# Both directions' state increments made in one block, the second one in a PSUM bank of the transposes

## The chip, the cores and the metric

One Trainium2 chip, one NeuronCore. The metric is the device time of one execution in microseconds. A core has TensorE (PE; its weight loads are PEld), VectorE (DVE), ScalarE (ACT), GpSimd (POOL) and SyncE (SP, whose queue issues the transfers). PSUM has eight banks, in which TensorE leaves its products.

## The reference

One layer of an encoder over 1024 and 512 tokens of width 1024. After an RMS norm one projection gives the columns of three mixers, whose outputs are joined and projected by w_out. The change lies in the third, a gated linear recurrence with four heads, run forwards and backwards and summed:

```python
def step(state, inp):
    qt, kt, vt, bt = inp                      # a chunk of tokens
    o = (einsum('bhts,bhsv->bhtv', scores, vt)
         + einsum('bhtk,bhkv->bhtv', qt * exp(bt), state))
    state = (exp(b_last)[..., None] * state
             + einsum('bhsk,bhsv->bhkv', kt * exp(b_last - bt), vt))
    return state, o
```

`o_f` runs over the tokens in order, `o_b` over the flipped ones; o = rmsnorm(o_f + o_b), times a gate.

## The kernel before, in words

**Tiling.** The 1536 tokens are three groups of 512. Groups 0 and 1 are one sequence, group 2 is another. In each of the four heads a group is a *unit*, made in the order 2, 0, 1 (`UNITS`). A unit has four chunks of 128 tokens (`NCH`). Projections (`project`, `project_tokens`; tiles pf, pq, pg, pi) are chains of matmuls of a high and a low part.

**Steps.** The code walks through the projections, and after every three matmuls of 512 columns (or six of 256) calls `step()`. It advances a clock by one and resumes those generators that are due. A generator's `yield n` means: resume n steps later. So the small work of the recurrence is put between projection matmuls, in an order fixed when the kernel is built.

**Who keeps that order.** A tile framework adds the semaphores and orders each engine's instructions by its own estimate of when they are ready. In the part with the four heads VectorE alone is held to the order of the code (`manual_schedule`). That part ends with the last gate projection of head 3, after which the output projection (tiles po, yh, yl, yx) begins.

**A unit's generators.** `scores` makes the product of queries and keys inside a chunk by levels m = 1, 2, 4, ... 64. Each level has matmuls (L819, L880; tiles sd, sc), a mask copy (L866 into L, L884 into A), updates of Q, K and T on VectorE (L794, L811), and copies kc, q on ScalarE (L800, L830). It yields 3 steps, then 5 four times, then 1. The next unit's `scores` begins one step after.

`states` first transposes the keys of both directions (tile tk, PSUM tag tp, two banks; copied to kt by ScalarE, L913), yields 4, then makes the increments: per chunk a matmul of keys and values, into a PSUM tile U. `advance` (L925, L928) chains them into the states S on VectorE, the factors coming from `tot` (L905). U's tag is uo, which has one bank. The forward increments are consumed first; `yield 3`; then the backward ones. If the unit isn't the last of its sequence, its last forward increment and its backward ones are copied aside (`keep`, `ub`) by ScalarE; if it is the last, the backward chain runs over all units of the sequence. In both cases the tiles are read by VectorE or ScalarE.

`output` starts 6 steps after the second increments: the product o (L986, the same bank uo), four squares on ScalarE (L991), an inverse root on GpSimd (tile sto, L118 and L119), and the normalised `on` on VectorE (L993). Eight steps later, if the gate G is there, it transposes `on` into a tile `to` (L999, tag tp) and VectorE multiplies by G into yc (L1001), which is stored.

In unit 2 of each head the states and output lie beside the scores of unit 0; in unit 1 no scores run.

**At the end of head 3** the tiles that held the group's activations are reused: the two halves of w_out are loaded into them as each gate projection is done with them (`load_w_out`), then the rows yx of the output projection (L1050).

**The other lines in the rows.** L776 is the gate G. L124 on GpSimd makes the low part wl of a weight, L791 the sum ks of the keys.

Of the kernel before, what the change touches and what calls it, by code (L numbers as in the profile page):

```python
# [15 lines left out]
AF = mybir.ActivationFunctionType  # L16
# [8 lines left out]
NCH = GRP // P  # L25
# [29 lines left out]
def trunk_kernel(ctx, tc, x_prompt, x_sample, norm_g, w_in, conv_w, conv_b, conv_ln_g, conv_ln_b,  # L55
# [3 lines left out]
    act = nc.scalar.activation  # L59
# [21 lines left out]
    def tp_t(name):  # L81
        return ps_tp.tile([P, GRP], F32, tag="tp", name=name)
# [7 lines left out]
    def uo_t(name):  # L90
        return ps_uo.tile([P, NCH, P], F32, tag="uo", name=name)

    def by_chunk(t):
        return t.rearrange("p (c n) -> p c n", c=NCH)
# [813 lines left out]
    def keys_transposed(u, d):  # L908
        tp = tp_t(f"tk{u['n']}{d}")
        for c in range(NCH):  # L910
            nc.tensor.transpose(tp[:, c * P:(c + 1) * P], u["K"][:, d, c * P:(c + 1) * P], ident)
        t = s2(f"kt{u['n']}{d}")
        act(t, tp, AF.Copy)  # L913
        return t

    def increments(u, d, kt, used):
        up = uo_t(f"U{u['n']}{d}")
        for c in used:
            nc.tensor.matmul(up[:, c, :], kt[:, c * P:(c + 1) * P], u["V"][:, c, :], start=True, stop=True)  # L919
        return up  # L920

    def advance(dst, prev, u, d, c, inc):

        if prev is None:
            dve.tensor_copy(dst, inc)  # L925
        else:
            t = u["tot"][:, d * NCH + c:d * NCH + c + 1]
            dve.scalar_tensor_tensor(out=dst, in0=prev, scalar=t, in1=inc, op0=ALU.mult, op1=ALU.add)  # L928

    def states(us, j):  # L930

        u = us[j]
        first, last = j == 0, j == len(us) - 1
        rp = rb["p"]
        while not u["prev"](2, "out"):
            yield 1
        u["S"] = rp.tile([P, 2, NCH, P], F32, tag="S", name=f"S{u['n']}", bufs=2)
        u["has"] = [[not (first and c == 0) for c in range(NCH)], [not (last and c == NCH - 1) for c in range(NCH)]]
        S = u["S"]
        kt0 = keys_transposed(u, 0)  # L940
        kt1 = keys_transposed(u, 1)
        u["turned"] = True
        yield 4
        while "V" not in u:
            yield 1
        up = increments(u, 0, kt0, range(NCH - 1) if last else range(NCH))
        if not first:
            p = us[j - 1]
            advance(S[:, 0, 0, :], p["S"][:, 0, NCH - 1, :], p, 0, NCH - 1, p["keep"])
        for c in range(NCH - 1):  # L950
            advance(S[:, 0, c + 1, :], S[:, 0, c, :] if u["has"][0][c] else None, u, 0, c, up[:, c, :])
        if not last:
            u["keep"] = rp.tile([P, P], F32, tag="keep", name=f"keep{u['n']}")
            act(u["keep"], up[:, NCH - 1, :], AF.Copy)
        yield 3
        up = increments(u, 1, kt1, range(1, NCH) if first else range(NCH))
        if not last:
            u["ub"] = rp.tile([P, NCH, P], F32, tag="ub", name=f"ub{u['n']}")
            act(u["ub"][:, 1:, :], up[:, 1:, :], AF.Copy)
            yield 2  # L960
            return
        prev = None
        for j in range(len(us) - 1, -1, -1):
            u = us[j]
            inc = up if j == len(us) - 1 else u["ub"]
            S = u["S"]
            if prev is not None:
                p, pinc = prev
                advance(S[:, 1, NCH - 1, :], p["S"][:, 1, 0, :], p, 1, 0, pinc[:, 0, :])
            for c in range(NCH - 1, 0, -1):  # L970
                advance(S[:, 1, c - 1, :], S[:, 1, c, :] if u["has"][1][c] else None, u, 1, c, inc[:, c, :])
            prev = (u, inc)
        yield 6
# [31 lines left out]
    def head(h):  # L1005
        us = un[h]

        def finish(gs, js):
            for j in js:
                yield from states([us[g] for g in gs], j)  # L1010
            if js[-1] == len(gs) - 1:
                for g in gs:
                    spawn(output(h, g, us[g]), 3 if g == 1 else 0)
                    yield 3

        for g in UNITS:
            us[g]["prev"] = lambda n, what, g=g: past(h, g, n, what)
            while "q" not in us[g] or not (past(h, g, 1, "scored") and past(h, g, 3, "out")):
                yield 1
            yield 1  # L1020
            yield from scores(us[g])
            if g == 2:
                spawn(finish((2,), (0,)), 2)
            elif g == 0:
                spawn(finish((0, 1), (0,)), 2)
        yield from finish((0, 1), (1,))
# [161 lines left out]
```

## Time and profile before

| what | value |
|---|---|
| median of 3 runs | 839.84 us (839.66 to 839.9) |
| the profiled execution | 840.24 us |
| its span, first to last instruction | 838.5 us |
| mean granted TensorE clock | 0.998 |
| TensorE busy | 819.5 us, 98% |
| VectorE busy | 490.7 us, 59% |
| ScalarE, GpSimd busy | 349.4 us, 278.0 us |

Times in the rows below are microseconds from the start of the span. A row of the timeline has the start, the duration from the first start to the last end of the merged instructions, the engine, the line, the operation, output and inputs, the shape, the count, and in brackets the idle time of the engine just before and what ended it. Matmuls are pipelined: several are in flight, so the time from one row's start to the next row's start says what a group costs. A 128x128 float32 product is shown as two matmuls.

### The profile page before, as it was taken

What the parts mean: (1) busy time and instruction counts of PE and PEld (TensorE: products, weight loads), DVE (VectorE), ACT (ScalarE), POOL (GpSimd) and SP (SyncE); (2) the same over time, 40 slices, a digit from 0 to 9 for tenths busy, and PEclk for the clock granted to TensorE, in tenths of its full rate; (3) what the DMA queues carried; (4) which work ended last, traced back from release to release, by engine and by line L of the source; (5) the groups of instructions that cost most, each with busy time, mean ns of one, the idle gap of its engine ahead of it and who ended that gap; (6) DMA issues with size and microseconds to landing.
All of it is one profiled execution on the core that took longest, in us unless ns stands there. A gap on an engine that the chain in (4) does not pass through costs nothing.

```text
span 838.5 us, 17608 instructions
## 1 busy us (share of the span) xinstructions
PE 819.5 (98%) x7249; PEld 702.2 (84%) x7249; DVE 490.7 (59%) x1024; ACT 349.4 (42%) x707; POOL 278.0 (33%) x288
## 2 busy tenths in 40 slices
PE   7999999999999999999999999999999999999996
PEld 6998898787788889988877788899888778888885
DVE  5737788876233488622478946885314888433332
ACT  5725547562343454522345433444223454222221
POOL 5827867999441320121221013212202010111111
PEclk9999999999999999999999999999999999999999
DMA  8404523434120200011110102001011594344421
GB/s 277 140 14 146 150 89 99 154 126 142 58 64 26 76 28 3 26 40 50 46 31 4 40 1 76 27 3 51 26 38 51 206 329 127 114 150 143 139 90 51
DMA packets 63842, 72.35 MB, mean 86 GB/s; under 512 B 3643, under 2 KB 46994, under 8 KB 62738
## 3 DMA queue, kind: packets, MB, share of 16 engines
q1 hardware_dynamic: 63762, 71.23, 25.8%
q8 instruction: 57, 0.93, 0.5%
q14 instruction: 23, 0.19, 0.1%
HBM read 50.25 MB, written 20.97 MB: 85 GB/s over the span
## 4 chain that ended last, share of the span: by engine, by line
PE 81%; DVE 8%; ACT 3%; POOL 3%; DMA 3%; issue 1%; SPq 0%; POOLq 0%; ACTq 0%; DVEq 0%
PE po L1072 5%; PE po L1074 5%; PE po L1073 5%; PE pf L205 5%; PE pf L207 5%; PE pf L206 5%; PE o L986 3%; PE pq L205 2%; PE pg L205 2%; PE sc L819 2%; DVE Q L794 2%; PE pq L206 2%; PE pg L206 2%; PE pq L207 2%; PE pg L207 2%; PE U L919 2%
## 5 line engine op out<-in xcount | busy, mean ns | idle before, releaser
L124 POOL TENSOR_TENSOR wl<-wr,wh 128x512 fp32r<-128x512 f32 x64 | 85.8, 1355 | 160.0 <-ACT wh L123 156.2
L476 DVE SCALAR_TENSOR_TENSOR ca<-glu,par,ca 128x512 f32<-128x512 f32 x120 | 80.6, 746 | 0.0
L1072 PE MATMUL po<-woh,yh 128*128 128x512 f32 (+1 forms) x200 | 77.4, 387 | 0.5 <-ACT yh L1052 0.5
L205 PE MATMUL pf<-hh,wh 128*128 128x512 f32 x192 | 76.8, 400 | 0.0
L1073 PE MATMUL po<-wol,yh 128*128 128x512 f32 (+1 forms) x200 | 76.2, 381 | 0.0
L1074 PE MATMUL po<-woh,yl 128*128 128x512 f32 (+1 forms) x200 | 76.1, 381 | 0.0
L207 PE MATMUL pf<-hh,wl 128*128 128x512 f32 x192 | 75.0, 391 | 0.0
L206 PE MATMUL pf<-hl,wh 128*128 128x512 f32 x192 | 74.8, 390 | 0.0
L800 ACT ACTIVATE kc<-K 128x512 f32<-128x512 f32 x84 | 56.3, 674 | 39.9 <-DVE K L794 36.5
L501 POOL TENSOR_TENSOR part<-part,pr 128x512 f32<-128x512 f32 x54 | 68.9, 1305 | 3.2 <-ACT pr L500 3.2
L794 DVE TENSOR_TENSOR Q<-Q,T 128x256 f32<-128x256 f32 x144 | 65.4, 495 | 2.7 <-ACT q L830 1.9
L123 ACT ACTIVATE wh<-wr 128x512 fp32r<-128x512 f32 x64 | 39.0, 627 | 53.1 <-PE pf L206 20.6
L794 DVE TENSOR_TENSOR K<-K,T 128x256 f32<-128x256 f32 x144 | 54.8, 422 | 5.8
L738 DVE TENSOR_SCALAR Q<-Q,oml,lbt 128x512 f32<-128x512 f32 x24 | 17.8, 742 | 64.7 <-ACT Q L735 60.7
L1078 DVE TENSOR_TENSOR yx<-po,yx 128x512 f32<-128x512 f32 (+1 forms) x25 | 16.7, 670 | 56.0 <-PE po L1074 56.0
L791 POOL TENSOR_TENSOR ks<-K 128x512 f32<-128x512 f32 x12 | 16.4, 1363 | 99.7 <-ACT kc L800 53.7
L1072 PEld LDWEIGHTS po<-woh,yh 128*128 128x128 f32 x200 | 37.6, 188 | 7.5 <-ACT yh L1052 0.7
L1074 PEld LDWEIGHTS po<-woh,yl 128*128 128x128 f32 x200 | 37.6, 188 | 7.4
L1073 PEld LDWEIGHTS po<-wol,yh 128*128 128x128 f32 x200 | 37.7, 188 | 6.9
L1090 POOL TENSOR_TENSOR stf<-stf 128x1 f32<-128x1 f32 x12 | 4.1, 341 | 117.6 <-ACT yx L1079 117.6
L207 PEld LDWEIGHTS pf<-hh,wl 128*128 128x128 f32 x192 | 36.0, 188 | 7.8
L205 PEld LDWEIGHTS pf<-hh,wh 128*128 128x128 f32 x192 | 36.1, 188 | 7.0
(366 smaller groups left out, 2275.3 us busy)
## 6 DMA issues: line engine op xcount, KB each, us to landing
wr<-in_w_in_dram SPq DMA_DIRECT2D x62, 256.0 KB
out_dram<-yx SPq DMA_DIRECT2D x24, 256.0 KB
yx<-yd SPq DMA_DIRECT2D x12, 448.0 KB
x<-in_x_prompt_dram SPq DMA_DIRECT2D x8, 512.0 KB
wor<-in_w_out_dram SPq DMA_DIRECT2D x16, 256.0 KB
wod<-woh SPq DMA_DIRECT2D x16, 256.0 KB
wod<-wor SPq DMA_DIRECT2D x16, 256.0 KB
woh<-wod SPq DMA_DIRECT2D x4, 1024.0 KB
```

The costliest lines, as they stand in the source:

```text
L123: act(hi, src, AF.Copy)
L124: pool_e.tensor_tensor(out=lo, in0=src, in1=hi.bitcast(F32), op=ALU.subtract)
L205: nc.tensor.matmul(pj[:, part], hi[:, k, :], hh, start=k == 0, stop=False)
L206: nc.tensor.matmul(pj[:, part], hi[:, k, :], hl, start=False, stop=False)
L207: nc.tensor.matmul(pj[:, part], lo[:, k, :], hh, start=False, stop=k == KT - 1)
L476: dve.scalar_tensor_tensor(out=acc, in0=src, scalar=col(R_CW + 2 * t + i), in1=acc, op0=ALU.mult, op1=ALU.add)
L501: pool_e.tensor_tensor(out=parts[g], in0=parts[g], in1=pr, op=ALU.add)
L794: dve.tensor_tensor(out=x, in0=x, in1=y, op=ALU.mult)
L800: act(view(kc, 0, [[2 * m, n2], [m, 2], [1, m]]), view(K, 0, [[2 * m, n2], [GRP + m, 2], [1, m]]), AF.Copy)
L1072: nc.tensor.matmul(po, yh[:, k, :], hi[:, ns], start=k == 0, stop=False)
L1073: nc.tensor.matmul(po, yh[:, k, :], lo[:, ns], start=False, stop=False)
L1074: nc.tensor.matmul(po, yl[:, k, :], hi[:, ns], start=False, stop=k == KT - 1)
```

## The change

The two calls of `increments` stand one behind the other, ahead of all `advance`. The backward one's tile comes from tag tp, the two banks of the transposes, and is called `ub` in the code. The `yield 3` between the two is gone.

```diff
     def increments(u, d, kt, used):
-        up = uo_t(f"U{u['n']}{d}")
+        up = uo_t(f"U{u['n']}{d}") if d == 0 else by_chunk(tp_t(f"U{u['n']}{d}"))
         for c in used:
             nc.tensor.matmul(up[:, c, :], kt[:, c * P:(c + 1) * P], u["V"][:, c, :], start=True, stop=True)
         return up
@@ def states
         up = increments(u, 0, kt0, range(NCH - 1) if last else range(NCH))
+        ub = increments(u, 1, kt1, range(1, NCH) if first else range(NCH))
         if not first:
             p = us[j - 1]
             advance(S[:, 0, 0, :], p["S"][:, 0, NCH - 1, :], p, 0, NCH - 1, p["keep"])
@@
         if not last:
             u["keep"] = rp.tile([P, P], F32, tag="keep", name=f"keep{u['n']}")
             act(u["keep"], up[:, NCH - 1, :], AF.Copy)
-        yield 3
-        up = increments(u, 1, kt1, range(1, NCH) if first else range(NCH))
         if not last:
             u["ub"] = rp.tile([P, NCH, P], F32, tag="ub", name=f"ub{u['n']}")
-            act(u["ub"][:, 1:, :], up[:, 1:, :], AF.Copy)
+            act(u["ub"][:, 1:, :], ub[:, 1:, :], AF.Copy)
             yield 2
             return
@@
-            inc = up if j == len(us) - 1 else u["ub"]
+            inc = ub if j == len(us) - 1 else u["ub"]
```

## Rows read from the trace of the kernel before

**Rows 1.** The page, part 1: busy time, share of the span, instructions.
```profile
PE 819.5 (98%) x7249; PEld 702.2 (84%) x7249; DVE 490.7 (59%) x1024; ACT 349.4 (42%) x707; POOL 278.0 (33%) x288
```
**Rows 2.** The view of tile U: its matmuls (duration min/median/max in ns, first and last start); then, under the head on idle time, that of TensorE's side; then who waited for it.
```profile
L919 PE MATMUL U<-V,kt x160: 270/275/377, 321.8 to 713.5; 128*128 128x128 f32 x160
...
  issue: 0.2, 1
...
  DVE S L925: 7.3, 6
```
**Rows 3.** Timeline of TensorE, head 0, the states of unit 2 and the first scores of unit 1 (only the first matmul of a projection stretch).
```profile
325.46 0.83 PE L919 MATMUL U<-V,kt 128*128 128x128 f32 x6
326.05 0.36 PE L229 MATMUL pi00a<-wh,hh 128*128 128x256 f32 x1
...
328.28 0.28 PE L229 MATMUL pi00a<-wh,hh 128*128 128x256 f32 x1
...
329.09 0.46 PE L880 MATMUL sc<-q,kc 128*32 128x32 f32 x32
...
331.62 0.39 PE L986 MATMUL o<-V,A 128*128 128x128 f32 x2
...
337.23 0.56 PE L819 MATMUL sc<-Q,kc 128*32 128x32 f32 x32
```
**Rows 4.** Timeline of VectorE in the same stretch.
```profile
330.21 0.74 DVE L884 COPY_PREDICATED A<-mk,sc 128x512 f32<-128x512 uint8 x1
...
333.18 1.29 DVE L794 TENSOR_TENSOR Q<-Q,q 128x512 f32<-128x512 f32 x2
336.61 0.69 DVE L993 TENSOR_TENSOR on<-o,sto 128x512 f32<-128x512 f32 x1 [2.14 <-POOL sto L119]
```
**Rows 5.** Timeline of GpSimd in the same stretch.
```profile
335.55 1.02 POOL L119 TENSOR_TENSOR sto<-sto,mexp 128x4 f32<-128x4 f32 x1
```
**Rows 6.** Timeline of VectorE, head 2, unit 2.
```profile
560.96 0.69 DVE L993 TENSOR_TENSOR on<-o,sto 128x512 f32<-128x512 f32 x1 [2.13 <-POOL sto L119]
```
**Rows 7.** Timeline of TensorE, head 1, from the scores beside unit 2's output to the first scores of unit 1.
```profile
453.10 0.46 PE L819 MATMUL sc<-q,kc 128*32 128x32 f32 x32
...
454.60 0.38 PE L986 MATMUL o<-V,A 128*128 128x128 f32 x2
...
460.08 0.69 PE L880 MATMUL sc<-Q,kc 128*64 128x64 f32 x16
...
462.87 1.03 PE L911 MATMUL tk<-ident,K 128*128 128x128 f32 x8
...
466.36 0.54 PE L819 MATMUL sc<-Q,kc 128*32 128x32 f32 x32 [0.23 <-DVE Q L794]
```
**Rows 8.** Timeline of VectorE in the same stretch.
```profile
454.23 0.29 DVE L866 COPY_PREDICATED L<-mk,sc 128x128 f32<-128x128 uint8 x1
...
456.52 0.76 DVE L794 TENSOR_TENSOR Q<-Q,T 128x256 f32<-128x256 f32 x2
...
459.71 0.69 DVE L993 TENSOR_TENSOR on<-o,sto 128x512 f32<-128x512 f32 x1 [1.49 <-POOL sto L119]
...
461.33 0.74 DVE L884 COPY_PREDICATED A<-mk,sc 128x512 f32<-128x512 uint8 x1
461.95 1.48 DVE L794 TENSOR_TENSOR Q<-Q,T 128x256 f32<-128x256 f32 x2
...
465.01 1.29 DVE L794 TENSOR_TENSOR Q<-Q,q 128x512 f32<-128x512 f32 x2
466.22 0.74 DVE L1001 SCALAR_TENSOR_TENSOR yc<-to,par,G 128x512 f32<-128x512 f32 x1
```
**Rows 9.** Timeline of GpSimd in the same stretch.
```profile
460.28 2.54 POOL L124 TENSOR_TENSOR wl<-wr,wh 128x512 fp32r<-128x512 f32 x2 [0.59 <-ACT wh L123]
```
**Rows 10.** Timeline of TensorE, head 3, from the last scores of unit 0 to the first matmul of the output projection.
```profile
682.53 0.46 PE L880 MATMUL sc<-q,kc 128*32 128x32 f32 x32
...
685.83 0.94 PE L919 MATMUL U<-V,kt 128*128 128x128 f32 x6
687.27 0.50 PE L1072 MATMUL po<-woh,yh 128*128 128x512 f32 x1 [0.50 <-ACT yh L1052]
```
**Rows 11.** Timeline of VectorE in the same stretch.
```profile
682.56 0.69 DVE L993 TENSOR_TENSOR on<-o,sto 128x512 f32<-128x512 f32 x1 [1.49 <-POOL sto L119]
683.17 0.75 DVE L794 TENSOR_TENSOR K<-K,Q 128x256 f32<-128x256 f32 x2
```
**Rows 12.** Timeline of SP's queue before that stretch: transfers as they are issued.
```profile
669.43 0.32 SPq L1036 DMA_DIRECT2D woh<-wod  x1
...
677.40 0.37 SPq L1050 DMA_DIRECT2D yx<-yd  x1
```
**Rows 13.** Timeline of ScalarE in that stretch.
```profile
686.26 0.95 ACT L1052 ACTIVATE yh<-yx 128x896 fp32r<-128x896 f32 x1 [0.89 <-DMA yx<-yd]
```
**Rows 14.** Timeline of VectorE, head 0, the backward chain of units 1 and 0.
```profile
361.38 0.29 DVE L925 COPY S<-U 128x128 f32<-128x128 f32 x1 [1.85 <-PE U L919]
...
362.86 1.13 DVE L928 SCALAR_TENSOR_TENSOR S<-S,tot,ub 128x128 f32<-128x128 f32 x3
```
**Rows 15.** Timeline of TensorE there.
```profile
365.75 0.39 PE L986 MATMUL o<-V,A 128*128 128x128 f32 x2
```

## The prediction

> **What bounds the kernel.** Three views, in this order. The page's busy times: TensorE is busy 819.5 us of 838.5 and VectorE 490.7 [rows 1], so time changes only where TensorE starts to wait, stops waiting, or gets other work. The view of tile U says whether the second product waits for its bank: the 160 matmuls into U cost TensorE 0.2 us of idleness, once, while VectorE stood 7.3 us before its copies out of U [rows 2]. So the wait that the old code could cause (bank uo holds one tile) is not there on TensorE: three projection steps are longer than the readers of the first product need. Then the timelines of TensorE, VectorE, GpSimd, ScalarE and SP around each head's states, to see what an earlier second product drags with it. Two things matter there: VectorE runs in code order in the part with the four heads, and the normalised output `on` stands in that order behind a long wait: in head 0 it starts at 336.61 after 2.14 us of waiting for GpSimd [rows 4], whose power instruction alone lasts 1.02 us [rows 5].
>
> **What is removed, added and moved.** *Matmuls.* None is added or removed. A block of six U rows takes 0.59 us to the next projection (325.46 to 326.05), whose first matmul is then shown as 0.36 us [rows 3] where later ones of this shape are 0.28 (the one at 328.28 [rows 3]). What a joined block saves, about 0.08 us at the restart, it loses by no longer hiding the last U matmul behind that restart. I take 0; bounds 0.08 us either way for twelve states, so 1.0 us both ways.
>
> *Three yields.* Removing `yield 3` moves everything behind it three steps forward. Three steps are 2.23 us of projection (326.05 to 328.28 [rows 3]). For the first unit of a pair only the ScalarE copy `ub` moves: nothing, since nothing waits for it before the pair's end. For the last unit of a sequence the output moves: o, its squares, `sto` and `on`.
>
> *Pairs (units 0 and 1).* No scores run beside the second unit's states. VectorE's last state update ends at 362.86 + 1.13 = 363.99 and o reads it at 365.75, 1.76 us later. The update chain loses its 1.85 us wait for the second product [rows 14] and ends near 362.1; o moves from 365.75 to about 363.2 [rows 15]. One us is left: cost 0, and if VectorE were busier than this it would be up to 1 us a head.
>
> *The single unit (2), heads 0 and 2.* Here the scores of the next unit run beside it. The code puts o six steps behind the second product. Before, that is two steps behind the group at L880; now it is one step ahead of it. In TensorE's order o (2.15 us) goes in front, from 331.62 to about 328.28. That costs TensorE nothing, it is the same work. But `on` goes in front on VectorE too: ahead of the mask copy into A (L884), the last Q update, tot and the whole start of the next unit's scores (K, T, Q times q), which before ran while o was being made. From o to `on` is 336.61 - 331.62 = 4.99 us [rows 3, 4], so `on` starts near 333.27. The next instruction starts 0.61 us after it (682.56 to 683.17 in head 3 [rows 11]), at 333.88. From A to the end of Q times q it took 330.21 to 334.47, 4.26 us [rows 4], which now ends at 338.14. The first scores of the next unit (L819, Q by kc) start at 337.23 [rows 3] and need it: before it was 2.8 us early, now 0.9 late. Queued behind: every DVE instruction of that unit's scores; for them waits TensorE's sc. Head 2 has the same wait of 2.13 us before `on` [rows 6] and gets the same 0.9. Bounds: 0, if the framework, which orders TensorE by its own estimate, lets projections go before these scores; 1.0 if not. It does reorder: in head 3 the sc matmuls of the next unit don't follow sd. But in heads 0 to 2 no group has left its place in the code, although the scores at 466.36 came 0.23 us late there [rows 7]. I take 0.9.
>
> *Head 1.* One step is 0.7 us, so o moves to two steps before the group at 453.10, about 451.66. Latency 459.71 - 454.60 = 5.11 [rows 7, 8]: `on` at 456.77, and the mask copy L866 at 457.38 instead of 454.23. The Q update ended 457.28, 3.05 us behind L866 [rows 8], so now near 460.4; the second part of sc L880 starts at 460.08 [rows 7], up to 0.3 late. Then a new wait: the transposed output `to` now comes before the next unit's key transposes, and the ring of two PSUM tiles reads tk, tk, U, to, tk, tk. The second of these tk takes the bank of `to` and waits for its reader yc, which VectorE reaches only after G, A, Q and tot. A starts at 461.33 now and near 461.5 then; Q behind it lasted 1.48 us for two, until 463.43, and tot follows, so yc runs 463.7 to 464.5. The second tk would start near 463.6 (462.87 for the pair, plus `to`): 0.9 late. These waits of TensorE don't add up, the last one counts: the scores at 466.36 started right behind Q times q, which ended at 466.30. yc (0.74) now stands ahead of that Q times q, not behind it, and A is 0.2 later: it ends between 467.0 and 467.2, 0.8 us later, and so do the scores. I take 0.8; bounds 0 (projections placed ahead) and 1.1.
>
> A rule bears on the 0.2 in it. The row: Q took 1.48 us for two [rows 8] while GpSimd ran two tensor_tensors from 460.28 to 462.82 [rows 9]. The Trainium skill, SBUF — State Buffer, § Who interferes with whom, says that a DVE instruction with two SBUF inputs contends with a GpSimd instruction that reads SBUF, and that the blocked one waits for the whole of the other. By that rule Q ends when GpSimd does, whatever its start, and a later A costs nothing behind Q: 0.7 in head 1. By the row's duration alone everything slides: 0.9.
>
> *Head 3.* Around 682.53 the projections are used up and TensorE fills time until yh arrives: it ran sc, tk, sd, to, U (at 685.83) and then waited until 687.27, where the trace shows 0.50 us for ScalarE [rows 10], which itself waited for the load of yx [rows 13]. With the second U in the first block, 0.6 us more can fill this gap. Against it: `on` in front delays the next unit's chain by about 3 us here as well, so sc and tk fall later in the gap, and the second tk waits for yc. The load issues: two of w_out at 669.43 hang on a projection that now stands behind the joined block, 0.7 us later; the yx load at 677.40 [rows 12] hangs on a projection that o now precedes, up to 2.2 us later. The yd load lands after those of w_out, so I count the 0.7. Plus 0.7, minus 0.6: 0; bounds -0.7 and +2.2.
>
> **Sum.** 0 + 0.9 + 0.9 + 0.8 + 0 = +2.6 us. The profiled execution took 840.24 us (span 838.5 and 1.7 around it), the median is 839.84, 0.4 below; so 842.4 us.
>
> **Rivals.**
> 1. *Not slower: the order absorbs it.* The framework sees that `on` holds VectorE up and places projections before sc and tk. For: it did so in head 3. Against: none of the 36 score groups in heads 0 to 2 was displaced. It decides if its estimate of o to `on` is near 5 us; if it counts GpSimd's power at 0.2 instead of 1.02, sc is held to be nearly ready and stays. Then only a few tenths remain: 840.0 us.
> 2. *Faster: the gap of head 3 is filled.* U goes into the wait before 687.27 (0.6) and head 1's late scores (0.23) come in time: 839.0, more if VectorE's lost wait for U (7.3 us in six places) lets scores come sooner. It needs the second tk copied before ScalarE turns to yh at 686.26.
> 3. *Slower still: the yx load.* It lands as much later as it is issued: +2.2 on top, 844.5. Against: until then the queue still carries w_out.
> 4. *The freed bank itself pays.* The Trainium skill, PSUM — Partial Sum Buffer, § Summary: rules for kernel authors, advises a different bank for what is read while matmuls run. By that rule the change should help. The row has 0.2 us of idle TensorE at U [rows 2]: 839.6 at best, the same within measurement.
>
> **Numbers.** Forecast 0.50, first rival 0.33, second 0.07, third 0.07, fourth 0.03. Within 0.2% (1.7 us, about what a measurement here can tell from no change): first, fourth, half the second, and 0.04 of the forecast where the stalls come out at half. So faster 0.04, same 0.43, slower 0.53. The range takes the partial absorption below and the bounds of heads 1 and 3 above: 839.3 to 844.0; the forecast's own is 841.3 to 843.5.
>
> **What would show it.** Right: in head 0 `on` on VectorE near 333.3 with 4 us of idleness before it, A behind it, and a wait of about 0.9 us before sc near 337.2; the same in head 2; in head 1 a wait before the second tk. Wrong: sc behind more projections and no wait (rival 1); `on` much sooner than 5 us after o; U inside the gap before po and po no later than 687.3 (rival 2).

## The result and the profile after

The changed kernel takes 846.21 us (median of 4 runs, 845.37 to 847.22) against 839.75 us of the kernel before in the same measurement: ratio 1.0074, 95% interval 1.0061 to 1.0087. It is slower by 6.5 us. The forecast was 842.4 us with a range of 839.3 to 844.0: the sign is right, the size is not, and the time lies outside the range. The profiled execution took 846.20 us, its span is 844.4, 5.9 more than before. In the rows below every line of the change's functions stands one number lower than before (L992 is `on`, L1000 is yc).

The page's first part, which answers [rows 1]: every engine has the same number of instructions, and TensorE is busy 1.6 us longer.

```profile
PE 821.1 (97%) x7249; PEld 703.4 (83%) x7249; DVE 489.5 (58%) x1024; ACT 348.3 (41%) x707; POOL 278.3 (33%) x288
```

The view of the waits of TensorE (in us: in total, times, longest), the kernel after. Before, the first line did not exist, and the second one read 2.1, 4, 0.7.

```profile
PE tk L911 <- DVE yc L1000: 3.6, 2, 2.0
...
PE sc L819 <- DVE Q L794: 3.5, 5, 0.9
```

Where the 5.9 us lie is found by taking the start of the same projection matmuls in both traces. The distances between them, in us, for all kernels of this study (worked out from the traces; the marks stand at 290.3, 383.3, 511.5, 607.6 and 682.2 in the kernel before, and the last of them is the last matmul of head 3's last gate projection; the runs e1 to e7 and e9 to e13 are told of below; "rest" goes from the last mark to the end of the span):

| kernel | to heads | head 0 | head 1 | head 2 | head 3 | rest | span |
|---|---|---|---|---|---|---|---|
| before | 290.33 | 92.94 | 128.23 | 96.13 | 74.58 | 156.24 | 838.5 |
| after | 290.12 | 93.94 | 131.59 | 97.12 | 74.49 | 157.16 | 844.4 |
| e1 | 290.08 | 92.94 | 128.14 | 96.12 | 74.55 | 156.33 | 838.2 |
| e2 | 290.51 | 95.82 | 135.52 | 98.98 | 75.41 | 159.42 | 855.7 |
| e3 | 290.35 | 92.95 | 128.12 | 96.11 | 74.60 | 155.58 | 837.7 |
| e4 | 290.00 | 93.96 | 129.35 | 97.13 | 74.59 | 156.98 | 842.0 |
| e5 | 290.37 | 93.95 | 131.63 | 97.09 | 74.85 | 158.64 | 846.5 |
| e6 | 289.45 | 93.94 | 128.42 | 97.10 | 74.49 | 157.05 | 840.5 |
| e7 | 291.03 | 94.58 | 128.83 | 97.72 | 74.56 | 156.54 | 843.3 |
| e9 | 290.37 | 92.80 | 128.86 | 96.48 | 75.08 | 156.57 | 840.2 |
| e10 | 290.62 | 93.95 | 130.34 | 97.12 | 74.88 | 157.03 | 843.9 |
| e11 | 291.98 | 92.91 | 128.14 | 96.10 | 74.94 | 156.40 | 840.5 |
| e12 | 291.12 | 93.63 | 129.38 | 96.93 | 74.61 | 156.96 | 842.6 |
| e13 | 290.44 | 92.00 | 127.21 | 95.16 | 74.60 | 155.33 | 834.7 |

After against before: +1.0 in head 0, +3.4 in head 1, +1.0 in head 2, +0.9 behind the last gate projection. The first column, in which all kernels have the same work, varies by 2.5 us from one execution to the next (289.45 to 291.98). A part of that is TensorE's clock: in the traces of e7 and of e10 to e13 the granted clock is about half for some 3.5 us between 13.5 and 24 us from the start, in the others it is not. Among kernels with the output in the same place, the column of head 3 varies by 0.4 us and the last one by up to 0.8, little less than the 0.9 that it shows here; the three columns of heads 0 to 2 repeat within about 0.1 us. So heads are compared by the columns. Each kernel's columns come from one execution.

**Head 0.** The timeline of TensorE (start, duration, engine, line, operation, shapes, count, and in brackets the idle time before and what ended it), which answers [rows 3]:

```profile
328.06 0.39 PE L985 MATMUL o<-V,A 128*128 128x128 f32 x2
...
338.06 0.54 PE L819 MATMUL sc<-Q,kc 128*32 128x32 f32 x32 [0.85 <-DVE Q L794]
```

VectorE in the same stretch, which answers [rows 4]:

```profile
333.06 0.69 DVE L992 TENSOR_TENSOR on<-o,sto 128x512 f32<-128x512 f32 x1 [3.53 <-POOL sto L119]
333.66 0.74 DVE L884 COPY_PREDICATED A<-mk,sc 128x512 f32<-128x512 uint8 x1
...
336.62 1.29 DVE L794 TENSOR_TENSOR Q<-Q,q 128x512 f32<-128x512 f32 x2
```

`on` starts 5.00 us behind o, VectorE stands 3.53 us ahead of it, and A, which was made at 330.21 before [rows 4], waits behind it until 333.66. Q times q ends at 337.91, and the first scores of the next unit begin at 338.06.

**Head 1.** VectorE, from the output to the next unit's Q times q; this answers [rows 8]:

```profile
457.38 0.69 DVE L992 TENSOR_TENSOR on<-o,sto 128x512 f32<-128x512 f32 x1 [2.43 <-POOL sto L119]
...
462.20 0.74 DVE L884 COPY_PREDICATED A<-mk,sc 128x512 f32<-128x512 uint8 x1
462.84 2.77 DVE L794 TENSOR_TENSOR Q<-Q,T 128x256 f32<-128x256 f32 x2
...
465.80 0.75 DVE L1000 SCALAR_TENSOR_TENSOR yc<-to,par,G 128x512 f32<-128x512 f32 x1
...
467.86 1.29 DVE L794 TENSOR_TENSOR Q<-Q,q 128x512 f32<-128x512 f32 x2
```

GpSimd beside it, which answers [rows 9]:

```profile
461.16 2.77 POOL L124 TENSOR_TENSOR wl<-wr,wh 128x512 fp32r<-128x512 f32 x2 [3.82 <-ACT wh L123]
463.88 1.45 POOL L791 TENSOR_TENSOR ks<-K 128x512 f32<-128x512 f32 x1
```

In the kernel before, GpSimd made ks (the sum of the next unit's keys) here:

```profile
453.74 1.28 POOL L791 TENSOR_TENSOR ks<-K 128x512 f32<-128x512 f32 x1 [15.64 <-ACT kc L800]
```

And TensorE there, which answers [rows 7]:

```profile
462.18 0.60 PE L998 MATMUL to<-ident,on 128*128 128x128 f32 x4
...
464.01 0.60 PE L911 MATMUL tk<-ident,K 128*128 128x128 f32 x4
...
466.61 0.87 PE L911 MATMUL tk<-ident,K 128*128 128x128 f32 x4 [2.00 <-DVE yc L1000]
...
469.97 0.59 PE L819 MATMUL sd<-q,ks 128*32 128x32 f32 x32
...
470.92 0.54 PE L819 MATMUL sc<-Q,kc 128*32 128x32 f32 x32
```

Head 1 begins 0.8 us later in this trace than in that of the kernel before, so A (462.20 against 461.33) and the first wl (461.16 against 460.28) are no more than 0.1 us late against the projections. But the two Q behind A take 2.77 us where they took 1.48 [rows 8]; the first one ends 0.3 us behind the second wl, the second one 0.3 us behind ks. In the kernel before, ks ran at 453.74, ahead of the output's inverse root; now it stands on GpSimd directly behind the two wl. So yc is late, and the second tk, whose bank `to` held, waits 2.00 us for it. Behind that wait, TensorE's granted clock is half for more than three microseconds. Some stretches of that time (length, then busy time of PE, PEld, DVE, ACT, POOL with their counts, PEclk, DMA share, GB/s), ahead of the second tk and behind it:

```profile
464.00:466.00 2.00, 0.61 (x5) 0.36 (x3) 1.97 (x5) 0.60 (x1) 1.33 (x1) 1.00 0.72 211
466.00:467.00 1.00, 0.39 (x3) 0.39 (x4) 1.00 (x3) 0.00 (x0) 0.00 (x0) 0.96 0.26 77
467.00:470.00 3.00, 3.00 (x13) 1.96 (x13) 2.12 (x4) 0.60 (x1) 0.00 (x0) 0.50 0.23 87
```

PEclk of 1.00 is 2.4 GHz, 0.50 is 1.2 GHz. At the lower level the projection matmuls follow each other at 0.43 us instead of 0.23. Before, the clock in this place was 1.00.

**Behind head 3's last gate projection.** TensorE, which answers [rows 10], and SP's issue of the yx load, which answers [rows 12]:

```profile
691.67 0.66 PE L911 MATMUL tk<-ident,K 128*128 128x128 f32 x4 [1.55 <-DVE yc L1000]
...
692.98 0.48 PE L1071 MATMUL po<-woh,yh 128*128 128x512 f32 x1
```
```profile
684.73 0.37 SPq L1049 DMA_DIRECT2D yx<-yd  x1
```

The load is issued 2.5 us ahead of the last gate matmul (687.26); before it was 4.8 us ahead (677.40 and 682.21). Yet nothing is seen to wait for it. ScalarE, which stood 0.89 us for the load before [rows 13], now makes yh without a pause, and is done 1.6 us ahead of po:

```profile
690.44 0.95 ACT L1051 ACTIVATE yh<-yx 128x896 fp32r<-128x896 f32 x1
```

What stands ahead of po on TensorE is the second tk, which waits for yc, and behind it the rest of sd and a part of U. From the last gate matmul to po it is 5.72 us, and 5.06 before.

### The profile page after: what moved, and what is told of

It reads as the page before. It is cut to its first block, busy times and chain, and to the rows that moved or that the text cites. A ratio compares the mean times of both kernels' runs of the same rounds, so it can differ in the third digit from the quotient of the medians.

```text
span 844.4 us, 17602 instructions
## 1 busy us (share of the span) xinstructions
PE 821.1 (97%) x7249; PEld 703.4 (83%) x7249; DVE 489.5 (58%) x1024; ACT 348.3 (41%) x707; POOL 278.3 (33%) x288
## 5 line engine op out<-in xcount | busy, mean ns | idle before, releaser
L794 DVE TENSOR_TENSOR Q<-Q,T 128x256 f32<-128x256 f32 x144 | 65.8, 498 | 2.4 <-ACT q L830 1.0
L794 DVE TENSOR_TENSOR K<-K,T 128x256 f32<-128x256 f32 x144 | 54.9, 421 | 5.7
L118 POOL TENSOR_SCALAR sto<-sto 128x4 f32<-128x4 f32 x12 | 2.3, 194 | 134.6 <-ACT on L990 134.6
L206 PEld LDWEIGHTS pf<-hl,wh 128*128 128x128 f32 x192 | 36.4, 190 | 7.0
```

What stands on the lines that cost most here:

```text
L206: nc.tensor.matmul(pj[:, part], hi[:, k, :], hl, start=False, stop=False)
L794: dve.tensor_tensor(out=x, in0=x, in1=y, op=ALU.mult)
```

## The experiments

**Is it the place of the output, the joined block, or the bank?** Three kernels. e1 leaves the block and the bank and puts the output back where it was, nine steps behind the block:

```diff
-        yield 6
+        yield 9
```

> The changed kernel, but the output of a sequence's last unit starts nine steps behind the joined increments instead of six, which is where it started before the change. Theory (the output's place in VectorE's order costs, neither the joined block nor the bank): 839.5 to 840.3 us, no wait of TensorE at tk, the first scores of unit 1 in heads 0 and 2 unhindered. Rival (the joined block or the bank of the transposes costs): 845 to 847 us.

Measured: 840.41 us, ratio 1.0004 (0.9995 to 1.0014). The columns of heads 0 to 2 are those of before within 0.1 us, and the others within what they vary by. The output's place is the whole loss.

e3 is the kernel before with only the bank changed:

```diff
-        up = uo_t(f"U{u['n']}{d}")
+        up = uo_t(f"U{u['n']}{d}") if d == 0 else by_chunk(tp_t(f"U{u['n']}{d}"))
```

> The kernel before with one edit: the second increments lie in a bank of the transposes; order and yields stay. Theory: 839.5 to 840.3 us, since TensorE had 0.2 us of idleness at U. Rival (the longer use of a transposes' bank makes tk or the transposed output wait): over 841.5 us, with waits of tk or to for S.

Measured: 839.58 us, ratio 0.9998 (0.9988 to 1.0007). The bank is worth nothing by itself, either way.

e2 is the kernel before with the output three steps earlier (`yield 3` instead of the last `yield 6`), and the increments still apart:

> The kernel before, two separate increments in the one bank, but the output starts three steps behind the second increments instead of six, so at the place that the change gave it. Theory: 845 to 847 us, with TensorE waiting about 1.0 us before the first scores of unit 1 in heads 0 and 2 and 2.0 and 1.6 us at tk in heads 1 and 3. Rival (block or bank): 839.5 to 840.3 us.

Measured: 857.1 us, ratio 1.0208 (1.0192 to 1.0223), far worse than expected. TensorE in head 0:

```profile
330.45 0.49 PE L986 MATMUL o<-V,A 128*128 128x128 f32 x2 [0.91 <-DVE S L928]
...
340.54 0.54 PE L819 MATMUL sc<-Q,kc 128*32 128x32 f32 x32 [1.13 <-DVE Q L794]
```

Here o stands only three steps behind the second increments, so it waits for VectorE's last S, and everything behind `on` is later by the same. Heads 0 and 2 lose 2.9 each; in head 1 (7.3 lost) a tk waits 2.6 us, and the granted clock is 0.50 in six microseconds behind it (472 to 478). The expectation had left out the time between the second U and o. So the joined block does do something: it is what lets o come early without waiting for S. What it buys is not wanted.

**Does the pair count?** e11 gives the old place to the single unit alone:

```diff
-        yield 6
+        yield 9 if len(us) == 1 else 6
```

> The changed kernel with the old place of the output (final yield 9) for the single unit 2 alone; the pairs (units 0 and 1) keep the early output (6). Theory (the pairs cost nothing, all of the loss is in the single unit): 840.0 to 840.6 us, as with 9 everywhere (840.41), and in the profile no wait of TensorE for o's S in the pairs. Rival (the early output costs in the pairs too, 0.3 us or more a head): 841.6 or more.

Measured: 841.15 us, ratio 1.0014 (1.0004 to 1.0023), 0.6 above the expected range and below the rival's. The columns of heads 0 to 2 are those of e1 within 0.03 us, so the pairs, in heads 0 to 2, cost nothing. The profiled execution, one of the slowest of its ten, has 1.9 us more than e1 ahead of the heads, with a stretch at half clock there (20.3 to 24.0 us), and 0.4 in head 3, which is what that column varies by. Where the 1.2 us of the median come from is not shown.

**Is it VectorE's order?** e7 puts the output two steps later than the change (`yield 8`), which is one step ahead of its old place.

> The changed kernel with the output two steps later (final yield of the states 8 instead of 6); the kernel with 9 took 840.41. Theory (what costs is what stands behind `on` in VectorE's order, and for how long): in heads 0 and 2 `on` now stands between tot and the next unit's K, T and Q times q. It can start only about 0.7 us before its old time (o one step before the old place, 5.0 us latency), so Q times q ends near 339.2 in head 0 and TensorE waits about 2.0 us for it, twice the 1.04 of the changed kernel; the same in head 2. In head 1 yc stands behind Q times q again: 0 to 0.5. Sum 840.4 + 2.0 + 2.0 + 0.3, and up to 0.8 in head 3: 844.7 (843.8 to 845.6). Rival (the loss shrinks with the distance that the output is moved ahead): a third of the changed kernel's loss, 842.3 us, with waits of less than 1 us in heads 0 and 2.

Measured: 844.94 us (843.88 to 845.27). Heads 0 and 2 lose 1.6 each, more than the changed kernel's 1.0, although the output is nearer to its old place. VectorE in head 0, and then TensorE:

```profile
336.62 0.69 DVE L992 TENSOR_TENSOR on<-o,sto 128x512 f32<-128x512 f32 x1 [4.03 <-POOL sto L119]
...
338.61 1.29 DVE L794 TENSOR_TENSOR Q<-Q,q 128x512 f32<-128x512 f32 x2
```
```profile
340.06 0.54 PE L819 MATMUL sc<-Q,kc 128*32 128x32 f32 x32 [1.24 <-DVE Q L794]
```

`on` now has only K, T and Q times q of the next unit behind it, less than in the changed kernel, but it starts 3.6 us later (336.62 against 333.06). The rival, a loss that shrinks with the distance, falls for these heads; the whole loss is smaller than the changed kernel's (844.94 against 846.21) because head 1 loses 0.6 and not 3.4. The price is set by what is queued behind `on` and by when `on` can start. Of the places tried (6, 8, 9 and, below, 12 steps) only the old one costs nothing; there the work that TensorE needs next is ahead of `on`.

e12 goes on to `yield 12`, three steps behind the old place:

> The changed kernel with the output six steps later (final yield 12), three behind its old place: `on` then stands behind five more instructions of the next unit's scores, and VectorE waits less for GpSimd's inverse root (2.1 us before `on` in the kernel before). Theory (that wait of VectorE costs TensorE nothing, since nothing that TensorE needs stands close behind it): 839.9 to 840.6, as with 9. Rival (VectorE's freed 2 us let the scores come sooner): 838.5 or less. Third (`to` or yc is late for the next tk or the store): 841 or more.

Measured: 844.40 us (843.75 to 846.28), a loss as in the third case, but not through `to` or yc. In heads 0 and 2 (0.7 and 0.8 us lost) the increments of the next unit, which take the bank of o, wait for `on`:

```profile
342.20 1.83 PE L919 MATMUL U<-V,kt 128*128 128x128 f32 x14 [0.55 <-DVE on L992]
```

In head 1 (1.2 lost) `on` waits 3.38 us with A, Q and Q times q behind it, and sc waits 1.45 us for them. So the old place is not merely late enough, it is between two costs.

**What makes head 1 cost 3.4?** e4 leaves o early but makes `to` as late as before (`yield 11` instead of `yield 8` ahead of it), so that it is behind both tk again.

> The changed kernel, but the transposed output comes eleven steps behind the output product instead of eight, so at the place it had before, behind the next unit's key transposes. Theory: the waits at tk in heads 1 and 3 (2.0 and 1.6 us) and the stretch at half clock behind the first go, the 1.0 us each in heads 0 and 2 stay: 841.5 to 842.5 us. Rival (the wait at tk is only the place where a late VectorE shows, and moves on to the next scores): 844 to 846 us.

Measured: 844.28 us (843.8 to 844.93), more than expected and inside the rival's range. In the columns head 1 has lost 2.2 of its 3.4, as expected; heads 0 and 2 keep their 1.0, and the rest keeps 0.7 of its 0.9. So the wait of tk is gone with all that follows from it, and what is left in head 1 is the wait for Q times q, as in the other heads:

```profile
468.25 0.54 PE L819 MATMUL sc<-Q,kc 128*32 128x32 f32 x32 [1.32 <-DVE Q L794]
```

So both sides of the expectation hold in part: the wait at tk goes, and a late VectorE shows at the next scores. But the run changes two things: GpSimd's ks moved as well, to 457.28, away from wl, and the two Q took 1.47 us. In the rest, where no tk waits any more, the output projection waits for yl instead:

```profile
692.71 0.50 PE L1073 MATMUL po<-woh,yl 128*128 128x512 f32 x1 [0.87 <-DVE yl L1052]
```

So behind the last gate projection two causes lie side by side, the tk and VectorE's late work ahead of yl, and taking away the one brings out the other.

e6 takes GpSimd's wl out of that place in the changed kernel; ScalarE writes zeros in its stead, so the result lacks this low part (the main lines of the edit):

```diff
+                if n == 23:
+                    act(hi[:, 4 * a:4 * a + 4, :], w_raw[2 * n + a], AF.Copy)
+                else:
                     split(...)
...
+            if n == 23: spawn(low_part(), 8)   # ScalarE: act(lo, hi, AF.Copy, scale=0.0)
```

> The changed kernel with the low part of one weight (number 23, the one that GpSimd makes from 461.16 to 463.93 in head 1) left at zero: ScalarE writes the zeros, GpSimd does not touch it. The sum of head 2's backward gates lacks that low part. Theory (the two Q updates behind A take 2.77 us instead of 1.48 because wl, wl and ks run back to back on GpSimd): the two Q take 0.8 to 1.5 us, the second tk of head 1 waits 0.7 us or less instead of 2.00, the granted clock stays at 1.00, head 1 costs about 1.1 and not 3.5, and the kernel takes 843.5 to 844.0 us. Rival (Q is slow for another reason, or GpSimd's ks alone does it): Q stays at 2.4 to 2.8, the wait at 1.7 to 2.0, the time at 845.9 to 846.4.

Measured: 843.58 us (842.32 to 845.02). ks runs at 456.71, and the Q behind A take a quarter of their time (in this kernel their line is L804):

```profile
462.52 0.74 DVE L804 TENSOR_TENSOR Q<-Q,T 128x256 f32<-128x256 f32 x2
```

The two tk are 0.3 us apart beyond their usual distance, the clock stays at 1.00, and head 1 costs 0.2. So of its 3.4 us, 3.2 need GpSimd beside Q. Three kernels give the scale: 2.77 us for the two Q with the second wl and ks beside them (the first wl has ended when Q begins), 1.47 with the second wl alone (e4), 0.74 with nothing.

**What does the slow clock cost?** e5 puts matmuls on the identity between the two tk of head 1:

```diff
         kt0 = keys_transposed(u, 0)
+        if us[0] is un[1][0] and j == 0:
+            warm(18)
         kt1 = keys_transposed(u, 1)
```

> The changed kernel with 18 matmuls of 128x128 on the identity, into the free bank uo, between the first and the second key transposes of unit 0 in head 1 (about 18 x 0.11 = 2.0 us of TensorE work where it now waits 2.00 us for yc). Their product is read by nobody. Theory (the wait itself costs 2.0, and the stretch at half clock behind it about 1.5 more): the granted clock stays at 1.00 behind the second tk, pf steps take 0.23 and not 0.43, and the kernel takes about 844.7 us, 1.5 less than the 846.2 of the changed kernel. Rival (the half clock only stretches work that would have waited anyway, for Q times q): the clock stays up and the time stays at 846.0 to 846.4. Third: the clock falls in spite of the fill, time unchanged.

Measured: 847.99 us (846.44 to 848.77). The fill was twice too long: each product shows as two matmuls, 36 in 4.0 us. TensorE there:

```profile
464.30 0.60 PE L911 MATMUL tk<-ident,K 128*128 128x128 f32 x4
464.74 4.18 PE L217 MATMUL warm<-ident 128*128 128x128 f32 x36
468.76 0.60 PE L911 MATMUL tk<-ident,K 128*128 128x128 f32 x4
...
472.94 1.28 PE L919 MATMUL U<-V,kt 128*128 128x128 f32 x10
```

The clock stayed at 1.00 in this place. From the first tk to U it is 8.64 us, and 8.64 in the changed kernel (464.01 to 472.65), although the second tk is 1.86 later: keeping TensorE at work gave back what the too long fill took, and head 1's column is the same. The kernel is slower than the changed one by 1.5 us in the last column. There the second tk of head 3 waits for yc as in the changed kernel (1.56 us against 1.55), but here the granted clock falls behind that wait:

```profile
692.32 0.66 PE L911 MATMUL tk<-ident,K 128*128 128x128 f32 x4 [1.56 <-DVE yc L1002]
```
```profile
694.00:697.00 3.00, 3.00 (x14) 2.76 (x13) 3.00 (x8) 1.61 (x3) 0.00 (x0) 0.55 0.90 242
```

So the last column does not speak about the fill. e10 halves the fill (`warm(9)`):

> The fill between the two key transposes of head 1 at half its size: each of the earlier 18 showed as two matmuls in the trace (36 of 0.112 us, 4.02 us instead of the 2.0 of the wait), so 9 now make 2.0 us. In that run the granted clock stayed at 1.00 and U began at the same place as in the changed kernel, although the second tk began 1.86 later: so the half-clock stretch is worth about 1.9. Theory: with a fill as long as the wait, the second tk starts where it did (about 2.0 behind the first), the clock stays at 1.00, the stretch from the second tk to U takes about 4.2 us instead of 6.0, and the kernel takes 844.3 to 844.8 us (846.2 less 1.6). Rival: the stretch is as long as before because sc waits for Q times q (ends near 469.2, so sc no sooner than that): then less than 0.5 is gained, 845.8 to 846.3.

Measured: 846.49 us (845.74 to 847.91). In the trace head 1 is 1.25 us shorter than in the changed kernel (130.34 against 131.59), with the clock at 1.00 and U 7.23 us behind the first tk:

```profile
464.59 0.60 PE L911 MATMUL tk<-ident,K 128*128 128x128 f32 x4
...
471.82 1.72 PE L919 MATMUL U<-V,kt 128*128 128x128 f32 x14
```

The times do not show it: the medians differ by 0.3 us the other way, and their ranges overlap. Head 1's column says 1.25 for the slow stretch in the one execution that was profiled; whether every execution of the changed kernel has that stretch, and that a kernel gains it as a whole, isn't shown.

**Can the kernel before be made faster?** e9 takes the waits that the kernel before has in heads 0 to 2 (0.78 to 0.86 us between sd and sc, 0.53 to 0.64 inside L880, counted from start to start beyond the usual distance) and gives the scores a step more at both places, the output two:

```diff
-        yield 3
+        yield 3 + 1 * early        # early: heads 0 to 2
...
-                yield LAGS[m]
+                yield LAGS[m] + 1 * (early and m == 64)
...
-        yield 6
+        yield 6 + 2 * (u['n'][0] != '3')
```

> A try at a better kernel, from the kernel before: in heads 0 to 2 the scores start one step later behind their Q times q (first yield 4 instead of 3) and the last level one step later (5 to 6), and the output follows two steps later (6 to 8), so that it keeps its place in VectorE's order. The kernel before has idle TensorE of 0.78, 0.86 and 0.78 us between sd and the first sc and of 0.53, 0.64 and 0.53 us inside the group at L880, 4.1 us in all, by the same reading that found the losses of the change. Theory (such a wait is worth its length, since projections are there to fill it): 836.0 to 837.5 us. Rival (the work that comes later stalls elsewhere, in the pairs or in head 3): 839.5 to 841.

Measured: 841.45 us, ratio 1.0020 (1.0011 to 1.0029): slower. The waits turn up elsewhere. Two of the waits of TensorE:

```profile
PE po L1073 <- ACT yh L1053: 0.8, 1, 0.8
PE U L920 <- ACT keep L955: 0.8, 1, 0.8
```

e13 goes to the cause instead. In the kernel before, wl, ks and wl run on GpSimd from 305.00 to 309.34 while VectorE makes the last Q and T of unit 2's scores in head 0, and the same stands in heads 1 and 2. There the two Q take 2.79 us (2.73 in head 1) and the T behind them 1.25. In head 0, before:

```profile
305.41 2.79 DVE L794 TENSOR_TENSOR Q<-Q,T 128x256 f32<-128x256 f32 x2
308.13 1.25 DVE L811 TENSOR_TENSOR T<-T 128x16 f32<-128x16 f32 x1
```
```profile
306.45 1.47 POOL L791 TENSOR_TENSOR ks<-K 128x512 f32<-128x512 f32 x1
```

e13 makes these two wl on VectorE (the main line of the edit; two helpers pass the engine on):

```diff
-                w_split()
+                w_split(dve if h < 3 else None)   # at the end of query(h)
```

> The kernel before, with one thing taken off GpSimd: the low part wl of the weight that is made at the end of each query projection of heads 0 to 2 (two tensor_tensors; 305.00 and 307.88 in head 0, with ks between them) is made on VectorE, two rows of about 0.68 us. In the kernel before, the two Q of that place take 2.79 us instead of 0.76 and the T behind them 1.25 instead of 0.17, in each of the three heads, and TensorE then waits 0.53 us inside L880 and 0.78 between sd and sc (0.64 and 0.86 in head 1). Theory (the same contention with GpSimd as in head 1 of the changed kernel, seen in the kernel before): only ks is left beside Q, Q takes about 1.5, T 0.17, Q times q ends about 1.1 us sooner in spite of the 1.36 us that VectorE gets, TensorE gains 0.9 to 1.3 in each of three heads, and the kernel takes 836.2 to 837.5 us. Rival (VectorE is the tight one, and the moved work costs what it saves): 839.4 to 840.4. Third (wl comes later and its first user waits): 841 or more.

Measured: 836.84 us (836.19 to 837.99) against 839.99, ratio 0.9965 (0.9951 to 0.9979). It is faster than both kernels. GpSimd, VectorE and TensorE in head 0:

```profile
299.50 1.29 POOL L791 TENSOR_TENSOR ks<-K 128x512 f32<-128x512 f32 x1 [10.81 <-ACT kc L800]
```
```profile
306.41 0.76 DVE L794 TENSOR_TENSOR Q<-Q,T 128x256 f32<-128x256 f32 x2 [0.42 <-ACT q L830]
...
308.08 1.29 DVE L124 TENSOR_TENSOR wl<-wr,wh 128x512 fp32r<-128x512 f32 x2
```
```profile
313.70 0.54 PE L819 MATMUL sc<-Q,kc 128*32 128x32 f32 x32 [0.15 <-PE sd L819]
```

With GpSimd free, ks moved 7 us ahead by itself, so Q takes 0.76 and not the 1.5 expected. VectorE got 1.29 us of work. Against that the two Q and T take 3.1 us less, while an earlier Q, at 299.71, now has ks beside it and takes 1.36 us instead of 0.42. Heads 0 to 2 are shorter by 0.94, 1.02 and 0.97 us, 2.9 together. The rest, another 0.9, is not claimed: e3 has nearly the same value there without any such change.

## Why the prediction was right, and where it failed

**Joined matmuls, 0: right.** e1 has the joined block in all twelve states and the columns of before. **Pairs, 0: right** (e11).

**Heads 0 and 2, 0.9 each: right, in mechanism and size.** The sum had o at 328.28, `on` at 333.27, Q times q ending at 338.14 and sc 0.9 late; the trace has 328.06, 333.06, 337.91 and, from sd to sc, 1.04 us more than before, and the columns say 1.0 and 1.0. That the framework leaves its place to sc, the choice between 0 and 1.0, was right too. e7 shows that it is VectorE's order and not the earliness that costs.

**Head 1, 0.8 (bounds 0 and 1.1): the failed step, 3.4.** With 3.4 in its place the sum alone would have left the range, at 845.0 us. The chain was right up to A: `on` 5.00 us behind o, `to` ahead of tk, the second tk waiting for yc. Then three statements were wrong.

First, the two Q: 1.48 us from [rows 8], or less if GpSimd's end sets theirs. Either way the prediction kept GpSimd's instructions where they were. But the framework orders GpSimd by its own estimate, and ks went from 453.74 to behind the two wl, which kept their place against the projections. That made 2.77 us, and 2.0 us of waiting at tk instead of 0.9. The Trainium skill has a rule for this in SBUF — State Buffer, § Who interferes with whom: a VectorE instruction with two SBUF inputs contends with a GpSimd instruction that reads SBUF, and the ports that the two share are an exclusive lock. The traces agree: each Q ends 0.3 us behind the GpSimd instruction beside it, and the pair takes 0.74 us where none is there. Weighing the rule, the prediction saw it absorb the lateness, with the two wl as the only GpSimd work beside Q; in fact ks had moved in behind them, and the same contention made the loss.

Second, "these waits of TensorE don't add up, the last one counts". The last one was to be Q times q. It ended at 469.15, but sc began at 470.92: in between TensorE was at half clock, working off projection matmuls ahead of it. In that execution the wait of 2.0 us had a price behind its end, 1.25 in head 1's column (e10), that neither a sum of waits nor the last wait holds.

Third, the bound of 1.1 was worked out only from VectorE's queue. With these two it was too narrow by 2.3, which is what put the time out of the range.

**Head 3, 0 (bounds -0.7 and +2.2): 0.8 together with the rest.** The load of yx is issued 2.3 us later against the last gate projection, as the upper bound had it, but nothing is seen to wait for it: yh is ready at 691.39, 1.6 us ahead of po. The second tk waits 1.55 us for yc, as said, and lies in the gap that was there before, so po comes 0.7 us later and not 1.55. The 0.6 us that a U was to fill in the gap were not gained: U stood behind the tk that waited. e4, in which no tk waits there, keeps 0.7 of the loss in a wait for yl, so no run shows what the tk alone costs.

**The rivals.** The order did not absorb anything on TensorE (rival 1); the framework did reorder, but GpSimd, and to the kernel's cost. The freed bank pays nothing (rival 4): in the Trainium skill, PSUM — Partial Sum Buffer, § Summary: rules for kernel authors, a different bank is advised for reading while matmuls run; e3 has only that, and 0.9998. Rival 3 had the later issue right, but not its cost: yh did not wait for the load.

## What to carry to other kernels

When an instruction is brought forward, look at what stands behind it on its engine's queue and when its input can be there: `on` was cheap only behind the work that TensorE needs next, and in heads 0 and 2 one step ahead of that place was worse than three. Where a framework orders some engines itself, an edit on one engine can move another engine's work; ask of each whether it ends up beside instructions that it blocks. And a VectorE row that is longer than its like in the same trace (2.79 against 0.76 us) is a place to look for time: moving GpSimd's work off it gave more than the steps that were set by hand.

## What was not expected of the hardware

TensorE's granted clock fell to 0.50 for more than 3 us behind a single wait of 2.0 us in the middle of a kernel whose mean is 0.997, and stayed at 1.00 where the wait was filled with 2.0 us of matmuls (e10). The length of the wait does not settle it: in head 3 the clock stayed at 1.00 behind 1.55 us in the changed kernel and fell behind 1.56 us in e5, and near the start of the span it stayed at 1.00 behind a wait of 1.70 us (at 18.96) in the kernel before and fell behind one of 1.70 (at 20.14) in e11. What decides is not shown.

The two engines slow each other both ways, and which of them began first shows. In heads 0 to 3 of both kernels a wl or ks that began while a K or Q (L794) ran on VectorE took 1.45 to 1.55 us; those that began ahead of a Q (wl at 462.63, and at 461.53 before) took 1.28 to 1.30, as in most other places. A Q that overlapped either went from 0.42 to as much as 1.5 us, so VectorE pays far more than GpSimd.
